# Attention scores: the low part of k meets only the high part of q, in pairs on the two halves of the array's rows

## The chip, the cores and the metric

The kernel runs on one core of a Trainium2 chip (trn2). The metric is the device time of one execution in microseconds. Its engines are TensorE (PE in the profile, its weight loads PEld), VectorE (DVE), ScalarE (ACT), GpSimd (POOL) and SyncE (SP), which here only issues DMAs.

## What is computed

A hybrid decoder block on 2048 tokens of width 1024, one layer: normalization with shift and scale, one large input product, a branch of sliding-window attention, a branch of chunked spatial gating, two gated projections, an output product and a second normalization. The change lies in the scores of the attention:

```
q = _rope(q.reshape(b, s, N_Q_HEADS, HEAD_DIM), positions)
k = _rope(k.reshape(b, s, N_KV_HEADS, HEAD_DIM), positions)
...
qb = q.reshape(b, nb, BLOCK, N_KV_HEADS, GQ, HEAD_DIM)
kb, vb = _band(k), _band(v)
scores = jnp.einsum('bnqkgd,bnjkd->bnkgqj', qb, kb).astype(jnp.float32)
scores = scores * (1.0 / math.sqrt(HEAD_DIM))
...
probs = jax.nn.softmax(jnp.concatenate([scores, sink], axis=-1), axis=-1)[..., :-1]
out = jnp.einsum('bnkgqj,bnjkd->bnqkgd', probs.astype(v.dtype), vb)
```

There are 8 query heads of width 64 on 2 key heads (4 query heads to each), blocks of 128 queries, and for each block the keys of its own and of the block before: 128 x 256 scores for each head. 2048 tokens are 16 blocks.

## The kernel before

Almost all of TensorE's work is large products (L163, in `mm3`). Every float32 operand is split into a high part in the type fp32r and a low remainder, and a product is three: high by high, high by low, low by high. The products run in *steps* of 12 matmuls of 512 columns each, and seven such steps (a product by Strassen's scheme, in banks X, Y, Z and W) make one block of outputs. The program is recorded in an order written out by hand: `later(n, f, post)` hangs a piece of other work before or after the matmuls of the n-th step from now, and each engine does its instructions strictly in the order in which they were recorded, with semaphores between the engines.

The attention of a block of 128 queries is a plan of such pieces (`att_block`), spread over 13 steps, one block every 8 steps. It runs twice, for the two halves of the sequence. For each of the two key heads `kv`:

- `load` fetches q and k from DRAM into tiles of the tag q. The tile of q has 128 partitions: 64 with the high part of the 64 head coordinates, and 64 with the low part; its four columns of 128 are the four heads g. The tile of k has the same content in both halves of its partitions: index 0 is the high part of k, index 1 the low part, 256 keys each.
- `scores` (at the end of a step) makes eight products into the two-bank tile `S`, of which there is one buffer. For each head g it multiplies the 128 rows of q (high above low) first by the high part of k (L907), then by the low part (L908), into the same 256 columns. Over 128 rows the sum is (high + low of q) by the part of k.
- `top` on VectorE masks and takes the maximum (L914 to L919), `exps` on ScalarE the exponentials (L927), `norm` (L936) the division, `trans` (L942) transposes on TensorE, and `masks` splits own and previous block.
- `pv`, once for both key heads, multiplies by v (L957) into the two halves of the output's partitions: its products have 64 columns of weights (128*64 in the profile).

The parts of q and k come from `ev_q` and `ev_kv`: `rope_finish` turns them, splits them into high and low, and `put_out` stores both parts to DRAM (L810 for q, index i of `q_s`: 0 high, 1 low).

The names of the profile's rows: `s` is the tile S, `q<-q` in a product reads tiles of the tag q (both k and q), `b` is a bank for small products, `m` a tile of the masked probabilities.

Of the kernel before, what the change touches and what calls it, by code (L numbers as in the profile page):

```python
# [55 lines left out]
def hybrid_block(ctx: ExitStack, tc: tile.TileContext, xt, x, wada, wgate, wI, wP, wO,  # L56
                 colc, rowc, bs, sinks, ws, pos, consts, mcp, out):
    nc = tc.nc
    act, dve, pool, pe, sp = nc.scalar, nc.vector, nc.gpsimd, nc.tensor, nc.sync
# [11 lines left out]
    def nm(s):  # L71
        uid[0] += 1
        return f"{s}_{uid[0]}"
# [484 lines left out]
    rows = {}  # L558
# [141 lines left out]
    def half(key):  # L700
        return int(key[1]) - 1

    def ft(key):
        return int(key[0]) - 1
# [38 lines left out]
    def rope_finish(h, R, put_out, wait):  # L743
        st = {}

        def turn():
            st["hi"] = flat("x", F32R)
            st["rot"] = st["hi"].bitcast(F32)
            for r in range(2):
                sp.dma_start(st["rot"][r:P:2, :], R[1 - r : P : 2, :])  # L750

        def mix():
            psub(st["rot"], st["rot"], ropet["s", h], ALU.mult)
            dve.tensor_tensor(out=R, in0=R, in1=ropet["c", h], op=ALU.mult)

        def both():
            add(R, R, st["rot"])
            act.copy(st["hi"], R)

        def low():  # L760
            sub(R, R, st["rot"])
        later(1 + wait, turn)
        later(5 + wait, mix)
        later(6 + wait, both, True)
        later(8 + wait, low)
        later(9 + wait, lambda: put_out(st["rot"], R))

    def rope_in(src, psum, tag):
        if not psum:
            return src  # L770
        R = flat(tag)
        act.copy(R, src)
        return R
# [30 lines left out]
    def ev_q(s, g0):  # L804
        def ev(key, src, psum):
            h, g = half(key), g0 + ft(key)

            def put_out(hi, lo):
                for i, t in enumerate((hi, lo)):
                    sp.dma_start(q_s[s][:, i, g, h * 512 : (h + 1) * 512], t)  # L810
            rope_finish(h, rope_in(src, psum, "x"), put_out, ("11", "22", "12", "21").index(key))
        return ev
# [66 lines left out]
    def att_block(b):  # L879
# [22 lines left out]
        def scores(kv):  # L902
            q, k = st.pop(("qk", kv))
            S = pS.tile([P, 2, 512], F32, tag="s", name=nm("s"))
            for g in range(4):
                o = S[:, g // 2, (g % 2) * 256 : (g % 2 + 1) * 256]
                pe.matmul(o, q[:, g, :], k[:, 0, :], start=True, stop=False)  # L907
                pe.matmul(o, q[:, g, :], k[:, 1, :], start=False, stop=True)  # L908
            st["S", kv] = S.rearrange("p b (k j) -> p (b k) j", k=2)

        def top(kv):
# [54 lines left out]
        for kv in range(2):  # L966
            t = 4 * kv
            plan += [(t - 3, False, lambda kv=kv: load(kv)), (t, True, lambda kv=kv: scores(kv)),
                     (t + 1, False, lambda kv=kv: top(kv)), (t + 2, False, lambda kv=kv: exps(kv, (0, 1))),
                     (t + 3, False, lambda kv=kv: exps(kv, (2, 3))), (t + 4, False, lambda kv=kv: recip(kv)),  # L970
                     (t + 4, False, lambda kv=kv: norm(kv, (0, 1))), (t + 5, False, lambda kv=kv: norm(kv, (2, 3))),
                     (t + 6, True, lambda kv=kv: trans(kv)), (t + 7, False, lambda kv=kv: masks(kv))]
# [381 lines left out]
```

## Time and profile before

| | |
|---|---|
| median of 3 runs | 1236.36 us (1235.69 to 1236.84) |
| the profiled execution | 1237.23 us |
| its span | 1235.5 us |
| mean granted TensorE clock | 0.993 |
| DMA: bytes moved, mean rate | 294.41 MB, 238 GB/s |

The page gives for each engine the busy time and its share of the span, and then the same in slices; the stretches in which the scores run are about 240 to 455 us and 658 to 870 us. In a row of a group stand line, engine, operation, out<-in, the active rows*columns of the array, shapes and the count, then busy time in us, the mean duration of one in ns, and the idle time of the engine ahead of them with what ended it. In a timeline a row is start, duration (both us), engine, line, operation, tiles, form and how many are merged. Matmuls are pipelined: a record's duration reaches beyond the start of the next one, so what one costs is read from the distance of starts.

These are the engines in 40 equal slices of the span, in tenths of busy time, and the TensorE clock granted:

```profile
PE   7788999999999999999999999999999999999997
DVE  6787789567767666348766675465756556777775
ACT  3587445476766677434345675455722112444443
PEclk9899999999999999999999999999999999999999
```

### The profile page before, as it was taken

What the parts mean: (1) busy time and instruction counts of PE and PEld (TensorE: products, weight loads), DVE (VectorE), ACT (ScalarE), POOL (GpSimd) and SP (SyncE); (2) the same over time, 40 slices, a digit from 0 to 9 for tenths busy, and PEclk for the clock granted to TensorE, in tenths of its full rate; (3) what the DMA queues carried; (4) which work ended last, traced back from release to release, by engine and by line L of the source; (5) the groups of instructions that cost most, each with busy time, mean ns of one, the idle gap of its engine ahead of it and who ended that gap; (6) DMA issues with size and microseconds to landing.
All of it is one profiled execution on the core that took longest, in us unless ns stands there. A gap on an engine that the chain in (4) does not pass through costs nothing. (4 is left out here: it accounts for less than half of the span.)

```text
span 1235.5 us, 17177 instructions
## 1 busy us (share of the span) xinstructions
PE 1202.1 (97%) x5494; PEld 959.3 (78%) x5494; DVE 831.2 (67%) x1288; ACT 620.2 (50%) x1340; POOL 269.9 (22%) x247
## 2 busy tenths in 40 slices
PE   7788999999999999999999999999999999999997
PEld 3466887878777777888888787777788888888886
DVE  6787789567767666348766675465756556777775
ACT  3587445476766677434345675455722112444443
POOL 1001556223456200013300001221000000135442
PEclk9899999999999999999999999999999999999999
DMA  9623998766999987478796666988787777854552
GB/s 346 256 77 127 311 334 295 243 185 212 298 341 339 297 298 266 147 225 293 254 281 185 176 183 187 345 252 261 262 295 230 227 247 241 265 179 143 164 179 85
DMA packets 215626, 294.41 MB, mean 238 GB/s; under 512 B 19888, under 2 KB 96304, under 8 KB 215536
## 3 DMA queue, kind: packets, MB, share of 16 engines
q1 hardware_dynamic: 215088, 292.39, 72.7%
q8 instruction: 43, 0.70, 0.2%
q0 software_dynamic: 304, 0.79, 0.2%
q14 instruction: 47, 0.39, 0.1%
q10 hardware_dynamic: 144, 0.13, 0.0%
HBM read 189.75 MB, written 98.24 MB: 233 GB/s over the span
## 5 line engine op out<-in xcount | busy, mean ns | idle before, releaser
L163 PE MATMUL bankY<-T,W 128*128 128x512 f32 x1608 | 390.6, 392 | 1.8 <-ACT bankZ L404 1.0
L163 PEld LDWEIGHTS bankY<-T,W 128*128 128x128 f32 x1608 | 299.4, 188 | 65.3 <-ACT bankZ L404 1.5
L146 DVE TENSOR_TENSOR W<-raw,W 128x512 fp32r<-128x512 f32 x323 | 239.9, 749 | 73.9 <-ACT W L207 73.9
L163 PE MATMUL bankX<-T,W 128*128 128x512 f32 x1140 | 281.0, 395 | 7.4 <-ACT T L614 4.9
L207 ACT CAST W<-raw 128x512 fp32r<-128x512 f32 x323 | 199.4, 618 | 154.7 <-PE b L163 58.0
L163 PEld LDWEIGHTS bankX<-T,W 128*128 128x128 f32 x1140 | 212.5, 189 | 53.4 <-ACT T L614 5.4
L163 PE MATMUL bankW<-T,W 128*128 128x512 f32 x708 | 175.8, 395 | 3.3 <-DVE T L146 2.6
L163 PE MATMUL bankZ<-T,W 128*128 128x512 f32 x708 | 171.1, 390 | 0.0
L163 PEld LDWEIGHTS bankW<-T,W 128*128 128x128 f32 x708 | 131.1, 189 | 35.1 <-DVE T L146 5.7
L163 PEld LDWEIGHTS bankZ<-T,W 128*128 128x128 f32 x708 | 132.2, 188 | 27.3
L149 POOL TENSOR_TENSOR S<-raw,raw 128x512 f32<-128x512 f32 x22 | 29.5, 1341 | 265.2 <-DMA raw<-m 200.3
L149 POOL TENSOR_TENSOR raw<-raw,raw 128x512 f32<-128x512 f32 x44 | 67.0, 1524 | 90.0 <-issue 39.2
L146 DVE TENSOR_TENSOR T<-x,T 128x512 fp32r<-128x512 f32 (+1 forms) x101 | 69.2, 723 | 14.3 <-ACT T L359 8.6
L152 DVE TENSOR_TENSOR e<-bankY,e 128x512 f32<-128x512 f32 x41 | 28.3, 690 | 65.8 <-PE bankY L163 65.2
L163 PE MATMUL s<-T,W 128*128 128x512 f32 x276 | 67.0, 390 | 1.6 <-DVE W L146 1.6
L149 POOL TENSOR_TENSOR S<-x,x 128x512 f32<-128x512 f32 x18 | 25.2, 1408 | 187.9 <-DMA x<-in_wO 178.5
L149 POOL TENSOR_TENSOR raw<-S,raw 128x512 f32<-128x512 f32 x22 | 32.7, 1488 | 139.9 <-DVE W L146 115.3
L163 PEld LDWEIGHTS s<-T,W 128*128 128x128 f32 x276 | 51.6, 188 | 12.7 <-DVE W L146 2.0
L359 ACT CAST T<-x 128x512 fp32r<-128x512 f32 x88 | 49.0, 618 | 4.3 <-PE s L163 4.2
L383 ACT COPY e<-bankW 128x512 f32<-128x512 f32 x41 | 24.0, 584 | 53.6 <-PE bankW L163 51.1
L404 ACT COPY bankZ<-bankY 128x512 f32<-128x512 f32 x42 | 24.0, 570 | 52.4 <-PE bankY L163 52.3
L936 ACT ACTIVATE P<-P,rc 128x128 f32<-128x128 f32 x128 | 44.5, 396 | 11.3 <-DVE rc L932 11.1
(226 smaller groups left out, 1403.2 us busy)
## 6 DMA issues: line engine op xcount, KB each, us to landing
raw<-in_wI SPq DMA_DIRECT2D x128, 256.0 KB, 4.4
raw<-sS SPq DMA_DIRECT2D x84, 256.0 KB, 4.3
g<-e SPq DMA_DIRECT2D x64, 256.0 KB, 3.8
sS<-raw SPq DMA_DIRECT2D x48, 256.0 KB, 4.0
T<-in_wada SPq DMA_DIRECT2D x16, 512.0 KB, 8.2
q<-q SPq DMA_DIRECT2D x64, 128.0 KB, 4.8
q<-k_s SPq DMA_DIRECT2D x64, 128.0 KB, 4.3
raw<-in_wP SPq DMA_DIRECT2D x32, 256.0 KB, 3.8
```

Source lines behind the costliest of these rows:

```text
L146: dve.tensor_tensor(out=o, in0=a, in1=b, op=ALU.subtract)
L149: pool.tensor_tensor(out=o, in0=a, in1=b, op=op)
L152: dve.tensor_tensor(out=o, in0=a, in1=b, op=ALU.add)
L163: pe.matmul(o, w[:, i, sl], t[:, j, kt, :], start=start and kt == kts[0] and n == 0, stop=stop and kt == last and n == 2, skip_group_check ...
L207: act.copy(w[:, 0, :], src)
L359: act.copy(T[p][:, 0, kt, :], rs[kt])
L383: act.copy(self.wsb, b["W"])
L404: act.copy(self.b[to], self.b[of])
L936: act.activation(out=st["P", kv][:, g, 0:P], in_=st["P", kv][:, g, 0:P], func=AF.Copy, scale=st["rc", kv][:, g : g + 1])
```

## The change

Two functions are edited.

```
@@ ev_q, put_out
-                for i, t in enumerate((hi, lo)):
+                for i, t in enumerate((hi, lo) if g < 2 else (lo, hi)):
                     sp.dma_start(q_s[s][:, i, g, h * 512 : (h + 1) * 512], t)
@@ att_block, scores
             S = pS.tile([P, 2, 512], F32, tag="s", name=nm("s"))
-            for g in range(4):
-                o = S[:, g // 2, (g % 2) * 256 : (g % 2 + 1) * 256]
-                pe.matmul(o, q[:, g, :], k[:, 0, :], start=True, stop=False)
-                pe.matmul(o, q[:, g, :], k[:, 1, :], start=False, stop=True)
+            o = [S[:, g // 2, (g % 2) * 256 : (g % 2 + 1) * 256] for g in range(4)]
+            for pair in ((0, 2), (1, 3)):
+                for g in pair:
+                    pe.matmul(o[g], q[:, g, :], k[:, 0, :], start=True, stop=False, skip_group_check=True)
+                for g in pair:
+                    rows = slice(64 * (g // 2), 64 * (g // 2 + 1))
+                    pe.matmul(o[g], q[rows, g, :], k[rows, 1, :], start=False, stop=True, skip_group_check=True)
```

For the heads g = 2 and 3 the tile of q now has the low part in its first 64 partitions and the high part in the last 64, since the two are stored the other way round. A product with the high part of k still takes all 128 rows, and there the order of the rows makes no difference to the sum. A product with the low part of k takes only the 64 rows with the high part of q: the first 64 for g = 0 and 1, the last 64 for g = 2 and 3. So the part low by low is no longer computed. The two products of a pair, g = 0 and 2 or g = 1 and 3, lie on different halves of the array's rows and write to different banks of S.

On TensorE this is the first call of `scores` with its neighbours. Before, L907 (high part of k) and L908 (low part) alternate:

```order
L163 MATMUL bankY<-T_988,W_2199 128x512 x12
L907 MATMUL s_2296<-q_2211,q_2208 128x256
L908 MATMUL s_2296<-q_2211,q_2208 128x256
L907 MATMUL s_2296<-q_2211,q_2208 128x256
L908 MATMUL s_2296<-q_2211,q_2208 128x256
L907 MATMUL s_2296<-q_2211,q_2208 128x256
L908 MATMUL s_2296<-q_2211,q_2208 128x256
L907 MATMUL s_2296<-q_2211,q_2208 128x256
L908 MATMUL s_2296<-q_2211,q_2208 128x256
L163 MATMUL bankX<-T_366,W_2231 128x512 x12
```

Now L909 is the product with the high part of k on 128 rows and L913 that with the low part on 64 rows (the shape given is that of the output, which stays 128 x 256):

```order
L163 MATMUL bankY<-T_988,W_2199 128x512 x12
L909 MATMUL s_2296<-q_2211,q_2208 128x256 x2
L913 MATMUL s_2296<-q_2211,q_2208 128x256 x2
L909 MATMUL s_2296<-q_2211,q_2208 128x256 x2
L913 MATMUL s_2296<-q_2211,q_2208 128x256 x2
L163 MATMUL bankX<-T_366,W_2231 128x512 x12
```

The number of products is the same; they stand in twos, and the division of the array changes four times where before it never changed. In 14 of the 32 calls the scores follow right behind `pv` (L957 before, L962 now), as here in the changed kernel:

```order
L962 MATMUL b_2716<-m_2514,v_2549 64x512
L962 MATMUL b_2716<-m_2669,v_2549 64x512
L962 MATMUL b_2716<-m_2515,v_2549 64x512
L962 MATMUL b_2716<-m_2670,v_2549 64x512
L909 MATMUL s_2721<-q_2599,q_2596 128x256 x2
L913 MATMUL s_2721<-q_2599,q_2596 128x256 x2
L909 MATMUL s_2721<-q_2599,q_2596 128x256 x2
L913 MATMUL s_2721<-q_2599,q_2596 128x256 x2
L163 MATMUL bankZ<-T_911,W_2628 128x512 x12
```

Here too the place of the call among its neighbours is unchanged. On SP the two stores of a q tile swap places for the heads 2 and 3; this is one such piece of the difference (x_1665 is the high part, x_1643 the low):

```order
 L238 DMA sS_0_106<-S_1823 128x512
 L238 DMA sS_2_108<-raw_1741 128x512
-L810 DMA q_284<-x_1665 128x512
-L810 DMA q_284<-x_1643 128x512
+L811 DMA q_284<-x_1643 128x512
+L811 DMA q_284<-x_1665 128x512
 L707 DMA za_262<-e_1855 128x512
```

No other instruction moves on any engine.

## Prediction

> **What bounds the kernel.** I read the page's head first, then the stages, then the waits of TensorE.
>
> ```profile
> span 1235.5 us, 17177 instructions
> PE 1202.1 (97%) x5494; PEld 959.3 (78%) x5494; DVE 831.2 (67%) x1288; ACT 620.2 (50%) x1340; POOL 269.9 (22%) x247
> ```
>
> TensorE (PE) is busy for 97% of the span and no other engine comes near it. The change touches only the attention scores, so the average counts for less than the two stretches in which the scores run. The view of busy time by stretches gives these two (from, to, then each engine's busy time):
>
> ```profile
> 235.00:480.00 245.00, 243.54 (x1177) 193.66 (x1176) 173.74 (x286) 163.35 (x397) 79.50 (x59) 1.00 0.86 278
> 650.00:900.00 250.00, 247.52 (x1185) 196.55 (x1184) 158.71 (x273) 145.67 (x365) 22.40 (x16) 0.99 0.75 231
> ```
>
> PE idles for 245.00 - 243.54 = 1.46 us in the first and 250.00 - 247.52 = 2.48 us in the second. The waits of PE name nearly all of that, and two of them stand at the scores themselves:
>
> ```profile
> PE s L907 <- DMA q<-k_s: 2.5, 1, 2.5
> PE s L907 <- ACT P L927: 1.2, 1, 1.2
> PE bankY L163 <- ACT bankY L404: 0.2, 1, 0.2
> ```
>
> So in these stretches PE sets the pace: whatever the scores take from it or give back to it, the end of the kernel gets, but for at most 3.9 us. The question is only what one call of `scores` costs on PE. These are the two lines of it, then one whole call, which lies between ordinary products of L163:
>
> ```profile
> L907 PE MATMUL s<-q,q 128*128 128x256 f32 x128 | 34.3, 299 | 3.7 <-DMA q<-k_s 2.5 <-ACT P L927 1.2
> L908 PE MATMUL s<-q,q 128*128 128x256 f32 x128 | 32.7, 287 | 0.0
> ```
>
> ```profile
> 242.92 0.28 PE L907 MATMUL s<-q,q 128*128 128x256 f32 x1
> 243.03 0.28 PE L908 MATMUL s<-q,q 128*128 128x256 f32 x1
> 243.15 0.28 PE L907 MATMUL s<-q,q 128*128 128x256 f32 x1
> 243.27 0.28 PE L908 MATMUL s<-q,q 128*128 128x256 f32 x1
> ...
> 243.75 0.28 PE L908 MATMUL s<-q,q 128*128 128x256 f32 x1
> 243.87 0.40 PE L163 MATMUL bankX<-T,W 128*128 128x512 f32 x1
> ```
>
> A product shows 0.28 us, but they overlap, and what one costs is the distance of the starts. From 242.92 to 243.87 eight products take 0.95 us, that is 0.119 us each. There are 128 + 128 of them, 32 calls of eight. All the 128 low products (L908) cost 128 x 0.119 = 15.2 us, and if every two of them shared one slot the gain would be at most half of it.
>
> **The change, part by part.** *Removed:* in each call the four low products become two pairs, each pair on the two halves of the rows. If the two of a pair run side by side, a pair costs one slot. The only packed products in this trace are those of L957, two at a time on the halves of the array's columns (128*64). For these the timeline shows, in windows that end behind the first record, the second and the last:
>
> ```profile
> 284.43 0.84 PE L163 MATMUL bankY<-T,W 128*128 128x512 f32 x3
> 284.88 0.39 PE L163 MATMUL bankY<-T,W 128*128 128x512 f32 x1
> 285.20 0.64 PE L957 MATMUL b<-m,v 128*64 128x512 f32 x1
> 285.20 0.65 PE L957 MATMUL b<-m,v 128*64 128x512 f32 x2
> 285.20 1.94 PE L957 MATMUL b<-m,v 128*64 128x512 f32 x8
> 287.07 0.39 PE L907 MATMUL s<-q,q 128*128 128x256 f32 x1
> 287.29 0.28 PE L908 MATMUL s<-q,q 128*128 128x256 f32 x1
> ```
>
> An unpacked product of the same width and type is L682; its two records are one instruction's:
>
> ```profile
> 131.64 0.59 PE L682 MATMUL b<-wT,ones 128*128 128x512 f32 x1
> 131.64 1.02 PE L682 MATMUL b<-wT,ones 128*128 128x512 f32 x2
> ```
>
> The second record of L682 begins at 131.64 + 1.02 - 0.59 = 132.07, so one slot is 0.43 us. Eight slots would be 3.44 us, but the eight records of L957 are past after 287.07 - 285.20 = 1.87 us, and the first two end 0.01 us apart (0.64 and 0.65): packed products do run in pairs, four slots for eight records. I take the same for halves of the rows. A pair then costs 0.119 + 0.01 us in place of 0.238, and a call gains 2 x 0.11 = **0.22 us**. The Trainium skill ("TensorE: Matmul & The Clock Gate", Part 3, Measured speedup vs the span model) puts the step from one packed tile to the next at about 4 ns; the 0.01 us here agrees within the rows' rounding, and by 4 ns a call would gain 0.01 us more.
>
> *Added:* a change between the whole array and its halves, four times a call (in, out, in, out), since the order is now two whole products, a pair, two whole products, a pair. The rows above show what such a change costs with halves of the columns. **Going in:** ordinary products start (284.88 - 284.43) / 2 = 0.225 us apart, but the first of L957 starts 285.20 - 284.88 = 0.32 us after the last whole one, 0.095 us late, and itself takes 0.64 instead of 0.59 us, another 0.05. **Coming out:** of the 1.87 us, four slots are 1.72 and the late first one 0.05, so 0.10 is left in which nothing starts. Then the first whole product is followed by the next after 287.29 - 287.07 = 0.22 instead of 0.12 us, another 0.10: coming out costs 0.20 us. The second part each time is a weight load that nothing covers, and it goes by the number of weight columns:
>
> ```profile
> L957 PEld LDWEIGHTS b<-m,v x128: 132/136/137, 285.2 to 894.1; 128*64 128x64 f32 x128
> L907 PEld LDWEIGHTS s<-q,q x128: 186/189/330, 242.7 to 870.0; 128*128 128x128 f32 x128
> ```
>
> The load of 64 columns takes 136 ns and that of 128 columns 189, 53 ns more; uncovered they cost 0.05 and 0.10. A tile of 64 rows still has 128 columns. So I take 0.095 + 0.10 = 0.195, rounded 0.20, for going in as well, and 0.145 (as measured for 64 columns) as its lower end. Four changes are 4 x 0.20 = **0.80 us** a call.
>
> No row shows halves of rows. From below, the change of the array's division could be free, since the products of L907 and L908 follow each other without any pause; from above, the two loads of a pair could come one after the other and be uncovered both, 0.10 more for each pair. I take the value of L957, the one row in which the array's division does change. The Trainium skill ("TensorEngine Tiling (Array Packing)", Tiling Modes, Key Properties) speaks against the change in the same sense: it says that a change of the tiling mode, as against a change from tile to tile within it, drains the engine. The trace agrees for the columns with the 0.095 and 0.10 us in which nothing starts; that the rule covers rows as well, no run before shows. By it the sum is the one below, without it the first rival.
>
> *The sum:* 0.80 - 0.22 = 0.58 us longer a call, 32 x 0.58 = **18.6 us**. Some calls follow L957 directly; there the first way out is paid already, and they still add their own four changes, as the first two products of a call are whole ones and so is what follows it.
>
> *Moved:* for the heads of the upper two tiles the stores of q swap their places, the same two transfers with the same bytes one behind the other; cost nothing. The low part of q still meets the high part of k in the whole products; low times low is left out, which takes no instruction away. No wait is added: only the first product of a call waits, as before. VectorE starts its reading of the scores (L915) when the last product is done:
>
> ```profile
> 288.33 0.70 DVE L915 COPY_PREDICATED s<-mcpt,s 128x512 f32<-128x512 int32 x1 [0.45 <-PE s L908]
> ```
>
> It starts 0.58 us later now, and the low parts of the weights stand behind it. VectorE has 245.00 - 173.74 = 71 us to spare in the first stretch, and none of the waits quoted above is one of PE for VectorE. So that is hidden; if the cover were gone, it would be 0.58 us a call again. The two waits at L907 could swallow some of what PE loses: 2.5 us at a transfer, if that transfer is not itself held up by PE. The 1.2 us behind ACT are not, since the exponentials of L927 come behind the scores before.
>
> The profiled execution took 1237.23 us (span 1235.5), 0.9 more than the median of 1236.36. Counted from the execution, 1237.2 + 18.6 = 1255.8; at the median it is **1255.0 us**, and that is what I give.
>
> **The rivals.**
>
> *Halves of rows need no pause (the other side: faster).* Place: the four changes of a call. If a pair's loads can be put under the whole products ahead of it, as those of L908 are put under L907 now, only the gain is left: 32 x 0.22 = 7.0 us, 1229.3. It decides from 0.055 us a change (0.22 / 4): below that the change is a gain. For it: whole products follow each other with no pause, and sub-tiles of rows keep all output columns in use. Against it: the 0.095 and 0.10 us at L957, both far above 0.055.
>
> *Only the pause, no uncovered load.* Four changes of about 0.10, so 0.40 - 0.22 = 0.18 a call, 5.8 us, 1242.1. Against it: the loads after the pause lie bare at L957 and at L907 behind it, 0.05 and 0.10.
>
> *The pairs don't run side by side, and the changes are paid.* Then nothing is gained: 32 x 0.80 = 25.6 us, 1262.0. The case of loads in series, 32 x (0.80 - 0.22 + 0.20) = 25.0, gives nearly the same. Against it: the pairs of L957.
>
> *Neither side by side nor paused:* 1236.4, nothing changed.
>
> **How the numbers follow.** Forecast 0.70, with a range of its own of 1249 to 1258: its low end has going in at 0.145 (2 x 0.145 + 2 x 0.20 - 0.22 = 0.47 a call, 15.0 us, 1251.4) less the 2.5 us of the wait. Free changes 0.14, the pause alone 0.08, serial pairs or serial loads with changes 0.05, neither 0.03. The range from 1239 to 1262 takes in the forecast, the pause alone and the serial case, 0.83, and leaves out 0.17. By over 0.2% (2.5 us, about what a measurement of this kernel can tell from no change) faster is the first rival, 0.14; within it the last, 0.03; slower the rest, 0.83.
>
> **What would show it.** In the timeline of a call after the change: the distance from the first whole product to the next L163, 0.95 us before, should be near 1.5; the two products of a pair should start within 0.01 us of each other; the start of a pair should come about 0.10 us later than 0.119 behind the whole product ahead, and its duration should be longer by about 0.10; the same for the whole product behind a pair. Busy PE should stay near 97%, since the pauses are shorter than what the records' overlap covers. I am wrong if the starts within a call stay 0.12 us apart at the changes: then the call is shorter by 0.22 us and the kernel faster. I am wrong in size if the first product of a pair isn't lengthened.

## The result

| | before | changed |
|---|---|---|
| median | 1236.55 us (4 runs, 1235.69 to 1236.84) | 1255.06 us (4 runs, 1254.63 to 1255.49) |
| ratio of the times | | 1.0153, 95% interval 1.0138 to 1.0168 |
| profiled execution, its span | 1237.23, 1235.5 us | 1255.11, 1253.4 us |

The changed kernel is 18.5 us slower. The page's head, to be held against that of before:

```profile
span 1253.4 us, 17178 instructions
PE 1224.0 (98%) x5494; PEld 962.7 (77%) x5494; DVE 829.0 (66%) x1288; ACT 620.6 (50%) x1340; POOL 270.4 (22%) x247
```

The span has grown by 17.9 us and busy PE by 21.9; no other engine has noticeably more to do. PE's waits are 4.0 us shorter in all, most of it outside the scores: the wait of L550 for POOL alone takes 1.7 us here and 4.2 in the trace of before. The stretches with the scores (now 235 to 490 and 665 to 920 us), columns as before:

```profile
235.00:490.00 255.00, 253.78 (x1178) 195.41 (x1177) 175.45 (x287) 163.96 (x398) 78.89 (x59) 0.99 0.83 269
665.00:920.00 255.00, 252.92 (x1164) 193.47 (x1163) 152.54 (x268) 144.61 (x363) 23.32 (x16) 0.99 0.72 225
```

PE idles for 1.22 and 2.08 us in them, hardly less than before (1.46 and 2.48), and for the same two reasons, as the waits of PE show:

```profile
PE s L909 <- DMA q<-k_s: 2.1, 1, 2.1
PE s L909 <- ACT P L932: 1.2, 1, 1.2
```

So what the calls take longer goes to the end. One call in the timeline, the answer to the eight rows of before; L909 is a product on the whole array, L913 one on half of its rows. The windows of this view end behind the first and the second record of each group:

```profile
301.93 0.28 PE L909 MATMUL s<-q,q 128*128 128x256 f32 x1
301.93 0.40 PE L909 MATMUL s<-q,q 128*128 128x256 f32 x2
302.25 0.38 PE L913 MATMUL s<-q,q 64*128 64x256 f32 x1
302.25 0.38 PE L913 MATMUL s<-q,q 64*128 64x256 f32 x2
302.57 0.38 PE L909 MATMUL s<-q,q 128*128 128x256 f32 x1
302.79 0.28 PE L909 MATMUL s<-q,q 128*128 128x256 f32 x1
303.00 0.39 PE L913 MATMUL s<-q,q 64*128 64x256 f32 x2
303.31 0.50 PE L163 MATMUL bankY<-T,W 128*128 128x512 f32 x1
```

The two of a pair start and end together (0.38 for one, 0.38 for both). The second whole product starts at 301.93 + 0.40 - 0.28 = 302.05, the pair 0.20 us behind it, where a product of this size is followed after 0.12: 0.08 to 0.09 late. And the pair lasts 0.38 instead of 0.28. On the way out the next whole product comes 0.32 us after the pair's start, that is 0.12 + 0.10 for the pair's own load + 0.10 pause, and it too lasts 0.38. Behind the second pair the longer record is that of L163, 0.50 against 0.40. From the first whole product to L163 the call takes 303.31 - 301.93 = 1.38 us, and the 0.10 in L163 belong to it: 1.48 against 0.95, **0.53 us a call**. Times 32 that is 17.0 us.

The weight loads of the halves, by line:

```profile
L909 PEld LDWEIGHTS s<-q,q x128: 186/188/333, 240.9 to 887.5; 128*128 128x128 f32 x128
L913 PEld LDWEIGHTS s<-q,q x128: 182/183/285, 241.4 to 887.8; 64*128 64x128 f32 x128
```

A load of 64 rows takes 183 ns, one of 128 rows 188: it goes by its 128 columns, not by its rows. That nothing covers the load behind a change can be read from where it starts. First a call before (its products start at 242.92 and 243.03), then the call above, the load of the second whole product and that of the first half:

```profile
242.69 0.19 PEld L907 LDWEIGHTS s<-q,q 128*128 128x128 f32 x1
242.92 0.19 PEld L908 LDWEIGHTS s<-q,q 128*128 128x128 f32 x1
301.93 0.19 PEld L909 LDWEIGHTS s<-q,q 128*128 128x128 f32 x1
302.25 0.18 PEld L913 LDWEIGHTS s<-q,q 64*128 64x128 f32 x1
```

An ordinary load starts together with the product ahead of its own (242.92 for the product of 243.03, 301.93 for that of 302.05) and runs under it. The load of L913 starts at 302.25, and the record of its own product starts there too.

### The profile page after: what moved, and what is told of

It is laid out like the page before. It is cut to its first block, busy times and chain, and to the rows that moved or that the text cites. A ratio compares the mean times of both kernels' runs of the same rounds, so it can differ in the third digit from the quotient of the medians.

```text
span 1253.4 us, 17178 instructions
## 1 busy us (share of the span) xinstructions
PE 1224.0 (98%) x5494; PEld 962.7 (77%) x5494; DVE 829.0 (66%) x1288; ACT 620.6 (50%) x1340; POOL 270.4 (22%) x247
## 5 line engine op out<-in xcount | busy, mean ns | idle before, releaser
L163 PE MATMUL bankY<-T,W 128*128 128x512 f32 x1608 | 391.9, 392 | 1.5 <-ACT bankZ L404 1.0
L163 PEld LDWEIGHTS bankY<-T,W 128*128 128x128 f32 x1608 | 299.6, 188 | 66.3 <-ACT bankZ L404 1.5
L146 DVE TENSOR_TENSOR W<-raw,W 128x512 fp32r<-128x512 f32 x323 | 236.8, 740 | 80.7 <-ACT W L207 80.7
L163 PE MATMUL bankX<-T,W 128*128 128x512 f32 x1140 | 282.7, 396 | 7.5 <-ACT T L614 5.0
L163 PEld LDWEIGHTS bankX<-T,W 128*128 128x128 f32 x1140 | 212.6, 189 | 54.9 <-ACT T L614 5.5
L163 PE MATMUL bankW<-T,W 128*128 128x512 f32 x708 | 178.6, 400 | 3.2 <-DVE T L146 2.4
L163 PE MATMUL bankZ<-T,W 128*128 128x512 f32 x708 | 171.5, 391 | 0.0
L163 PEld LDWEIGHTS bankW<-T,W 128*128 128x128 f32 x708 | 132.6, 191 | 36.4 <-DVE T L146 5.6
L163 PEld LDWEIGHTS bankZ<-T,W 128*128 128x128 f32 x708 | 132.2, 188 | 27.9
L163 PE MATMUL s<-T,W 128*128 128x512 f32 x276 | 67.0, 390 | 1.0 <-DVE W L146 1.0
L163 PEld LDWEIGHTS s<-T,W 128*128 128x128 f32 x276 | 51.6, 188 | 12.0 <-DVE W L146 1.4
```

The costliest lines, as they stand in the source:

```text
L146: dve.tensor_tensor(out=o, in0=a, in1=b, op=ALU.subtract)
L163: pe.matmul(o, w[:, i, sl], t[:, j, kt, :], start=start and kt == kts[0] and n == 0, stop=stop and kt == last and n == 2, skip_group_check ...
```

## The experiments

The theory: every change between the whole array and its halves costs about 0.194 us (a pause of some 0.09 and a weight load of some 0.10 that nothing covers), and two products on different halves share one slot. All kernels are compared with the kernel before on the same chip. The edits are given against the changed kernel.

**whole_rows** keeps the new order, banks and stores, and takes only the halves away.

```
-                    rows = slice(64 * (g // 2), 64 * (g // 2 + 1))
+                    rows = slice(0, P)
```

> The order of products, the two stores of q and the two-and-two of the banks are those of the changed kernel, but the low products take all 128 rows again. Theory (each change between the whole array and its halves costs about 0.195 us, each call has four, and its two pairs win back 0.23): no change of division is left and nothing is won, so 1236.5, as before. Rival (the loss comes from the new order, from alternating banks or from the swapped stores): 1255, as in the changed kernel.

Measured 1236.57, ratio 1.0003 (0.9992 to 1.0014). The order, the two-and-two of the banks and the swapped stores cost nothing; the whole loss lies in the division of the array.

**same_half** keeps the four changes and takes away that the two of a pair run side by side.

```
-                for i, t in enumerate((hi, lo) if g < 2 else (lo, hi)):
+                for i, t in enumerate((hi, lo)):
...
-                    rows = slice(64 * (g // 2), 64 * (g // 2 + 1))
+                    rows = slice(0, 64)
```

> The four low products take 64 rows, but all of them the first 64, and q is stored as before. Theory: the four changes stay (4 x 0.194 = 0.776 us a call) and the 0.23 us of running side by side go, so 32 x 0.776 = 24.8 more than before, 1261.3; inside a pair the starts lie 0.12 us apart. Rival (the pairs win nothing, or it is the switch itself that serializes them): 1255, as in the changed kernel.

Measured 1259.62, ratio 1.0195 (1.0175 to 1.0215). The call in the timeline:

```profile
301.74 0.40 PE L909 MATMUL s<-q,q 128*128 128x256 f32 x2
302.07 0.50 PE L913 MATMUL s<-q,q 64*128 64x256 f32 x2
302.50 0.50 PE L909 MATMUL s<-q,q 128*128 128x256 f32 x2
302.93 0.50 PE L913 MATMUL s<-q,q 64*128 64x256 f32 x2
303.36 0.96 PE L163 MATMUL bankY<-T,W 128*128 128x512 f32 x3
```

Two products on the same half end 0.50 - 0.38 = 0.12 us apart, those on different halves together, and the call up to L163 takes 1.62 instead of 1.38. So the pairs do win, 0.24 us a call by this row, 7.7 us in 32 calls; the times give 5 us against the first measurement of the changed kernel (ratio 1.0153) and 7 against its repetition further down (1.0137). The four changes alone cost some 24 us.

**two_changes** makes the four whole products first and then both pairs.

```
-            for pair in ((0, 2), (1, 3)):
-                for g in pair:
-                    pe.matmul(o[g], q[:, g, :], k[:, 0, :], start=True, ...)
-                for g in pair:
+            for g in (0, 2, 1, 3):
+                pe.matmul(o[g], q[:, g, :], k[:, 0, :], start=True, ...)
+            for g in (0, 2, 1, 3):
```

> The same eight products, but the four whole ones first and then the two pairs: two changes a call in place of four. Theory (cost per change): 2 x 0.194 - 0.231 = 0.157 us a call over before, 32 x 0.157 = 5.0, so 1241.5; the second pair starts 0.12 us after the first. Rival (cost per pair, as loads of 64 rows can't be covered, or the write to the bank just written has to be waited for): still 1255.

Measured 1241.63, ratio 1.0043 (1.0028 to 1.0058). In this kernel the second head of a bank starts its sum before the first head's is finished, so that for heads 0 and 2 the low product overwrites the whole one instead of adding to it (what the output shows of this stands in the last section); the instructions are the same eight. **one_start_two** mends that: only the first product in a bank starts a sum.

```
-                pe.matmul(o[g], q[:, g, :], k[:, 0, :], start=True, ...)
+                pe.matmul(o[g], q[:, g, :], k[:, 0, :], start=g in (0, 2), ...)
```

> The order with two changes again, but only the first product in each bank starts a sum, so that the second head's start no longer clears the mark of the first head's sum. The instructions are the same eight, so theory (cost per change) gives the same time as that run, 5.0 over before, 1241.5. Rival (the time of that run was low because products of heads 0 and 2 overwrote instead of adding): nearer to 1255.

Measured 1240.55, ratio 1.0034 (1.0022 to 1.0046), and its call:

```profile
299.40 0.40 PE L908 MATMUL s<-q,q 128*128 128x256 f32 x2
299.73 0.50 PE L911 MATMUL s<-q,q 64*128 64x256 f32 x4
300.16 3.00 PE L163 MATMUL bankY<-T,W 128*128 128x512 f32 x12
```

(The first row begins behind the call's first two products, as the window does.) The four halves end within 0.50 us where one pair ended within 0.38: the second pair costs 0.12, no pause and no bare load. With two changes taken away, about 14 of the 18.5 us are gone: the price hangs on the changes, not on the pairs.

**pairs_first** turns this round, the pairs ahead of the whole products. (Here the order of the starts makes the high products of heads 0 and 2 overwrite the low ones.)

```
-            for pair in ((0, 2), (1, 3)):
...
+            for g in (0, 2, 1, 3):
+                rows = slice(64 * (g // 2), 64 * (g // 2 + 1))
+                pe.matmul(o[g], q[rows, g, :], k[rows, 1, :], start=True, ...)
+            for g in (0, 2, 1, 3):
+                pe.matmul(o[g], q[:, g, :], k[:, 0, :], start=False, ...)
```

> The two pairs first, then the four whole products. Theory with a change from halves of columns to halves of rows at the price of any other change: in the 18 calls behind a whole product 0.157 us over before as in the last run, in the 14 behind the products of the probabilities by v one change only is added, 0.194 - 0.231 = -0.037; sum 18 x 0.157 - 14 x 0.037 = 2.3, so 1238.8. Rival (from columns to rows costs two changes, as if by way of the whole array): 1241.5, as in the last run.

Measured 1235.99, ratio 0.9997 (0.9986 to 1.0009). The time is 2.8 us below the forecast, which lies outside the interval. The calls themselves are as forecast: behind the products by v (L960 here) and behind L163

```profile
285.12 1.03 PE L960 MATMUL b<-m,v 128*64 128x512 f32 x4
286.07 0.51 PE L909 MATMUL s<-q,q 64*128 64x256 f32 x4
286.51 0.74 PE L911 MATMUL s<-q,q 128*128 128x256 f32 x4
287.09 0.40 PE L163 MATMUL bankZ<-T,W 128*128 128x512 f32 x1
...
299.49 0.50 PE L909 MATMUL s<-q,q 64*128 64x256 f32 x4
299.92 0.74 PE L911 MATMUL s<-q,q 128*128 128x256 f32 x4
300.50 0.62 PE L163 MATMUL bankY<-T,W 128*128 128x512 f32 x2
```

a call takes 287.09 - 286.07 = 1.02 us behind L960, where before it took 288.13 - 287.07 = 1.06: 0.04 less. So from halves of columns to halves of rows costs one change, not two. Behind L163 it takes 1.01, and it starts 0.09 late, 0.15 more than before. Some 18 x 0.15 - 14 x 0.04 = 2.1 us were to be seen, and why the time doesn't show them stays open. In this trace the wait for k_s is 1.5 us where it was 2.5 before, which could hide 1.0 of them; but in the trace of whole_rows, with the time of before, it is 3.2, so one trace doesn't settle it.

**mixed** takes pairs first only where the scores follow the products by v (key head 1 of all blocks but the first of each half), and the old code elsewhere; again the high products of heads 0 and 2 overwrite in those calls.

```
+            if kv == 1 and b % 8 > 0:
...
+            else:
+                for g in range(4):
+                    pe.matmul(o[g], q[:, g, :], k[:, 0, :], start=True, stop=False)
+                    pe.matmul(o[g], q[:, g, :], k[:, 1, :], start=False, stop=True)
```

> Pairs first in the 14 calls that follow the products by v, the old eight whole products in the other 18. Theory: 14 x (-0.045), as those calls were 1.015 us long against 1.060 in the run with the pairs first: 0.6 less than before, 1235.6, which the measurement can hardly tell from no change. Rival (the run with the pairs first came out 2.8 us below its forecast because something else got faster by it): 1233 or less.

Measured 1236.77, ratio 0.9996 (0.9985 to 1.0006): no change that can be told, and not the 1233 that a hidden gain of the last kernel would have given. **one_start_mixed** is the same with one start for each bank.

```
-                    pe.matmul(o[g], q[rows, g, :], k[rows, 1, :], start=True, ...)
+                    pe.matmul(o[g], q[rows, g, :], k[rows, 1, :], start=g in (0, 2), ...)
```

> The mixed kernel with one start for each bank: pairs first behind the products by v, eight whole products in the other calls. Theory: 14 x 0.046 = 0.6 less than before, 1235.8, not to be told from no change; in the trace the 14 calls take 1.014 against 1.060 us and the others 0.953. Rival (adding onto the pairs' sums costs what overwriting didn't): the 14 calls take 1.06 or more.

Measured 1235.71, ratio 0.9999 (0.9990 to 1.0008). A call behind the products by v (L965 here):

```profile
284.70 1.94 PE L965 MATMUL b<-m,v 128*64 128x512 f32 x8
286.57 0.51 PE L910 MATMUL s<-q,q 64*128 64x256 f32 x4
287.01 0.74 PE L912 MATMUL s<-q,q 128*128 128x256 f32 x4
287.58 2.68 PE L163 MATMUL bankZ<-T,W 128*128 128x512 f32 x11
```

287.58 - 286.57 = 1.01 us, as without the mending. Of the orders tried that leave out no more than low by low, this is the cheapest place for the halves, and it is a tie with the kernel before.

**eight_changes** alternates whole and half for each head.

```
+            for g in (0, 2, 1, 3):
+                rows = slice(64 * (g // 2), 64 * (g // 2 + 1))
+                pe.matmul(o[g], q[:, g, :], k[:, 0, :], start=True, ...)
+                pe.matmul(o[g], q[rows, g, :], k[rows, 1, :], start=False, ...)
```

> The eight products in the order whole, half, whole, half and so on: eight changes of division a call, no two halves side by side. Theory (every change costs about 0.194 us, however many there are): 8 x 0.194 = 1.55 us a call, 32 x 1.55 = 49.7 over before, 1286. Rival (a fixed cost of each call that uses halves at all, or the price falls when a change follows right behind another): at most the 25 us of four changes without pairs, 1261 or less.

Measured 1286.11, ratio 1.0394 (1.0377 to 1.0412).

```profile
305.69 0.28 PE L909 MATMUL s<-q,q 128*128 128x256 f32 x1
305.90 0.38 PE L910 MATMUL s<-q,q 64*128 64x256 f32 x1
306.21 0.38 PE L909 MATMUL s<-q,q 128*128 128x256 f32 x1
...
307.78 0.38 PE L910 MATMUL s<-q,q 64*128 64x256 f32 x1
308.09 0.50 PE L163 MATMUL bankY<-T,W 128*128 128x512 f32 x1
```

Every product behind a change starts 0.31 us after the last: 0.12 for that one, 0.10 for its bare load, 0.09 pause. The call is 308.09 - 305.69 + 0.10 = 2.50 us, (2.50 - 0.95) / 8 = **0.194 us a change**. By the row of same_half four changes cost (1.62 + 0.10 - 0.95) / 4 = 0.19 each: between four and eight changes a call, with one or two products between them, the price simply adds up.

**halves_only** stays in one division for the whole call, at the price of work left out.

```
+            for pair in ((0, 2), (1, 3)):
+                for j in range(2):
+                    for g in pair:
+                        rows = slice(64 * (g // 2), 64 * (g // 2 + 1))
+                        pe.matmul(o[g], q[rows, g, :], k[rows, j, :], start=j == 0, ...)
```

> This kernel leaves out the low part of q times the high part of k: the high products too run on 64 rows, in pairs, so a call is four pairs in one division, kh(0,2), kl(0,2), kh(1,3), kl(1,3), with one change at each end. Theory (tile to tile inside one division is free, only the change costs): 0.192 + 4 x 0.122 + 0.197 = 0.877 us against 0.952, and 0.195 less where the call follows the products by v; 18 x (-0.075) + 14 x (-0.27) = -5.1, so 1231. Rival (each pair pays an uncovered load, whatever it follows): three pairs more at 0.10, 9.6 us more, 1241.

Measured 1231.00, ratio 0.9958 (0.9942 to 0.9973). All eight products lie in one row of the timeline:

```profile
298.64 0.39 PE L163 MATMUL bankW<-T,W 128*128 128x512 f32 x1
298.96 0.74 PE L911 MATMUL s<-q,q 64*128 64x256 f32 x8
299.63 0.97 PE L163 MATMUL bankY<-T,W 128*128 128x512 f32 x3
```

From the first pair to L163 it is 0.67 us: four pairs at 0.12, 0.10 for the bare load of the first and 0.09 of pause behind the last. From one tile to another inside the division nothing is paid. With the pause ahead (0.32 instead of 0.23 behind L163) and the bare load in L163 the call costs 0.67 + 0.09 + 0.10 = 0.86 us, where eight whole products take 0.95.

**after_again** is the changed kernel a second time.

> The changed kernel once more, beside the others on the same chip: 18.5 us over before again, 1255. If the stretches of halved clock behind waits, of which its first trace has two more in the attention's part than that of before, belong to the change, they are at the same places again; if not, the trace has others, and the sum of the calls alone (0.54 us each, 17.2 in all) is what stays.

Measured 1253.95, ratio 1.0137 (1.0122 to 1.0151). The question was what the changed kernel's first trace has beyond its calls. In the view by stretches (the third number from the end is the granted clock) the changed kernel has, about its two waits,

```profile
271.18:274.59 3.41, 3.41 (x14) 3.11 (x13) 3.31 (x8) 1.09 (x3) 1.14 (x1) 0.50 0.30 100
800.24:807.07 6.83, 6.83 (x19) 4.97 (x20) 2.33 (x5) 0.00 (x0) 0.01 (x1) 0.50 1.09 357
```

half the clock in both, where the kernel before has

```profile
271.18:274.59 3.41, 3.41 (x23) 2.99 (x22) 3.38 (x7) 0.48 (x3) 0.44 (x1) 1.00 0.25 83
787.52:790.94 3.42, 3.37 (x12) 3.11 (x13) 1.22 (x3) 0.00 (x0) 0.04 (x1) 0.50 1.04 393
```

the full clock in the first and one such stretch of 3.42 us in the second. A stretch of 3.41 us at half clock does 1.7 us of work, so two more of them are up to 3.4 us. In the second trace of the changed kernel the first wait ends at 272.07, and the clock is full from before it to the second wait:

```profile
64.84:802.12 737.28, 726.91 (x3348) 574.59 (x3346) 495.77 (x785) 421.42 (x911) 180.20 (x147) 1.00 0.75 240
802.12:805.53 3.41, 3.41 (x10) 2.59 (x10) 2.33 (x5) 0.00 (x0) 0.00 (x0) 0.50 1.08 338
805.53:808.95 3.42, 3.42 (x17) 2.79 (x16) 0.69 (x1) 1.82 (x6) 0.00 (x0) 1.00 1.07 353
```

Only one stretch is left, as before the change. Other kernels differ as much: whole_rows, whose calls take what they took before, has two stretches at its wait for k_s, and mixed none:

```profile
787.77:794.59 6.82, 5.83 (x18) 5.00 (x19) 2.33 (x5) 0.00 (x0) 0.31 (x1) 0.50 1.09 357
780.00:800.00 20.00, 18.49 (x91) 14.12 (x90) 7.84 (x15) 9.20 (x26) 5.42 (x4) 1.00 1.08 360
```

So the two stretches don't always come with the change. Whether it makes them more frequent, these single traces don't show. The repetition is 16.9 us over the kernel before (1.0137 x 1236.43 = 1253.4), near the 17.2 of the calls alone.

## Why the prediction was right

The forecast was 1255.0 in a range of 1239 to 1262, with 0.83 on slower; measured 1255.06.

- *PE sets the pace in the stretches of the scores.* Right: PE idles there no more than before, and 0.53 us a call come out as 17 to 18 us of span. The wait for k_s, which could have swallowed up to 2.5 us, went from 2.5 to 2.1 in the first trace.
- *Two products on different halves share a slot.* Right, and shown by same_half against the changed kernel. The second follows at once (0.38 for one and for both), closer than the 0.01 us that was put in. The prediction calls the products of L957 the only packed ones of the trace; those of L566, ahead of the scores, are packed on halves of the columns too and agree (at 45.65 us the first lasts 0.64 instead of 0.59, and at 58.40 us the L163 behind the last lasts 0.50 instead of 0.40).
- *A change costs 0.20 us each way, as with the halves of columns.* Right in mechanism and size: 0.194 by eight_changes. The choice between 0.145 and 0.195 for going in, by the columns of the load and not by its rows, is borne out by the 183 ns of L913. The Trainium skill ("TensorEngine Tiling (Array Packing)", Tiling Modes, Key Properties) says that a change of the tiling mode drains the engine and a change of tile alone does not. The runs agree, for rows as for columns: 0.194 us a change in eight_changes, and nothing from pair to pair in halves_only, where a pair takes 0.12.
- *The sum.* 0.58 a call was put in and 0.53 came out. 0.024 of the difference is the rounding of 4 x 0.194 to 0.80, the rest the pairs and the rows' two decimals. So the calls account for 17.0 us (17.2 with the third decimal) of the 18.6 forecast, and the measured 18.5 hold 1.3 to 1.5 us more that the steps did not contain. Where these come from is not shown: the interval of the ratio, 1.0138 to 1.0168, reaches down to 17.1 us, the first trace has two more stretches of half clock, and the repetition came out at 16.9 us. That the forecast met the median to 0.1 us is therefore luck; its steps were good to 1.6 us.
- *The signs.* The distance from the first whole product to L163 was to be near 1.5 us and is 1.38. The last bare load, 0.10, lies in the record of L163 and not in this distance; the sign should have been put at 0.95 + 0.58 - 0.10 = 1.43, and the other 0.05 is the difference of the sum.
- *VectorE's later start is hidden.* Right: no wait of PE for VectorE stands in those stretches. The swapped stores are free (whole_rows).
- *The rivals.* Free changes fall with eight_changes, the pause alone with the bare loads in every trace, serial pairs with same_half. The point of balance of 0.055 us a change, given for the first rival, is little more than a quarter of what a change costs.

## What to carry to other kernels

Packing small products onto parts of the array pays only when enough of them stand together: here a pair saves 0.12 us, and going into the divided array and out of it costs 0.39, so by these numbers at least four pairs in a row are needed, and a call of `scores` has two. In halves_only four pairs in a row do come out ahead of eight whole products, by 0.09 us, though that kernel leaves out a part of the scores. These prices are of this case, products of 256 columns at full clock. Before writing such a change, look in the trace for any place where the array is already divided, by rows or by columns: the distances of the starts at its edges give the price of a change, and the uncovered load goes by the columns of the weights. If halves have to stand alone, put them next to another divided stretch, where they share an edge; in this kernel that gave a tie.

## What the runs showed of the hardware that was not expected

- Halves of rows directly behind halves of columns cost one change and not two (1.02 us against 1.06 for the call in pairs_first).
- In two_changes, where two heads of one bank both start their sums before adding to them, the output is off from the reference by 0.02195 of its size. A calculation with the reference alone gives the same number when the products of heads 0 and 2 with the high part of k are left out. With one start for each bank (one_start_two) this is gone, in the same time. The Trainium skill ("PSUM — Partial Sum Buffer", The four PSUM rules) describes this: a starting product clears the marks of the whole bank, and the next product of the other sum overwrites.
- Stretches of half clock of 3.41 us follow some waits of PE of 1.2 to 2.5 us and not others of the same length: behind the wait of 1.2 us at about 270 us the clock is 0.50 in the first trace of the changed kernel, and 1.00 in its second and in that of before. What decides between them, no run here shows.
